# The inner dimension of two FFNs in 45 tiles of 126 instead of 44 tiles of 128

## The chip, the core and the metric

The kernel runs on one core of one Trainium2 chip. The metric is the device time of one execution in microseconds (us). The kernel before the change took 2538.53 us, the median of three runs (2537.65 to 2539.0). In the views of the profile PE is TensorE's matmuls, PEld its weight loads, DVE is VectorE, ACT is ScalarE, POOL is GpSimd and SP the engine that issues most of the DMAs.

## The reference

One layer of a decoder for 320 tokens (256 of a prompt and 8 sequences of 8): a half-step FFN, a mixer of two kinds of heads, cross attention over 256 memory tokens, a second half-step FFN and a last norm. The change touches the two FFNs:

```python
def swiglu_ffn(x, wg, wu, wd):
    return (jax.nn.silu(x @ wg) * (x @ wu)) @ wd

def block(x, mk, mv, s0, buf0, lb, p):
    ...
    x = x + FFN_RES * swiglu_ffn(rmsnorm(x, n_f1), f1_g, f1_u, f1_d)
    m, s_new, buf_new = mixer(rmsnorm(x, n_mix), s0, buf0, lb, w_in, gnorm, conv_w, conv_b, ln_g, ln_b, w_out)
    x = x + m
    x = x + cross_attn(rmsnorm(x, n_xa), mk, mv, xa_q, xa_o)
    x = x + FFN_RES * swiglu_ffn(rmsnorm(x, n_f2), f2_g, f2_u, f2_d)
    return x, s_new, buf_new
```

x has 2048 columns (D_MODEL), the inner dimension of the FFNs (D_FF) is 5632, and everything is float32.

## The kernel before

Activations lie transposed: the 2048 columns of x are 16 blocks (KT) of 128 partitions by 320 tokens (T), the tiles xs. Every large product is made of three matmuls on float32r operands: a number is split into a high part (a cast to float32r) and a low part (the rest), and high x high, high x low and low x high are added up in PSUM. `mm3` issues the three (lines 206 to 208): the stationary operand is a 128 x 128 block of weights, its high part `whi` twice and its low part `wlo` once, and the moving operand is the high or low part of the activations, 128 x 320. Each matmul has its own weight load.

The weights of the whole program lie in one array in DRAM in the order in which they are used, cut into units of 128 x 1024, that is eight blocks. `unit` hands out the next one; `fetch` keeps four in work: a DMA into one of three buffers `raw` (512 KB, issued by SP), a cast to `whi` on ACT (line 136) and a subtraction to `wlo` on DVE (line 137).

`ffn` computes one FFN in parts of the inner dimension, PARTS = [8, 8, 8, 8, 8, 4] tiles of 128, 44 (FT) in all. For each tile, `strip` runs 16 blocks of gate weights (two units, 48 matmuls) against the pairs `xg` into a PSUM tile `acc`, `gate` scales it and applies Silu, a second strip does the same for the up weights, and `up` multiplies both and splits the product into the pair `hh`, `hl`. When the tiles of a part are there, the down projection runs for each of the 16 blocks n of the output over the part's tiles, and a DVE instruction (line 323) adds half of it to xs[n]. In the last part the first two blocks n are begun without the last tile and finished when it is there, which gives the last tile's gate and up time. The first five strips of the first FFN are run together by `first_strips` while x arrives, block by block over all five.

The order on each engine comes from the scheduler of the framework, with priority for the fetches; `first_strips` and PE in the end of the first FFN stand in the order in which they are written. There (`close`) the 16 tiles of the memory tokens are prepared between the tiles of the last part; they take pairs of the same 16 buffers as `hh`.

On the host, `strips` cuts gate and up weights into blocks, `downs` the down weights, and `ffn_groups` puts them in the order of use.

Of the kernel before, what the change touches and what calls it, by code (L numbers as in the profile page):

```python
# [10 lines left out]
F32 = mybir.dt.float32  # L11
# [3 lines left out]
ALU = mybir.AluOpType  # L15
AX = mybir.AxisListType

P = 128
DM = 2048
KT = DM // P  # L20
FF = 5632
FT = FF // P
NP = 256
NS = 64
T = NP + NS
# [10 lines left out]
XCUTS = ((0, 1), (1, 2), (2, 4), (4, 6), (6, 8), (8, 12), (12, 16))  # L36
HEAD = 5
EPS = 1e-6
PARTS = [8, 8, 8, 8, 8, 4]
LEVELS = [(0, T), (1, T), (2, T), (4, T), (8, NP), (16, NP), (32, NP)]  # L40

V_NORM = {"ffn1": 0, "mix": 16, "xattn": 32, "mem": 48, "ffn2": 64, "final": 80}
# [9 lines left out]

CRATE = 1.5
HRATE = 1.15


OUTPARTS = [list(range(7)), list(range(8, 16)) + [7]]
# [22 lines left out]
def hymba(tc, A, O):  # L80
# [3 lines left out]
    def tl(pool, shape, dt, tag, bufs):  # L84
        count[0] += 1
        return pool.tile(shape, dt, tag=tag, name=f"{tag}_{count[0]}", bufs=bufs)
# [9 lines left out]
    with (  # L96
# [8 lines left out]
        def acc():  # L105
            return tl(pp, [P, 512], F32, "acc", 4)
# [93 lines left out]
                mms[0] -= pace[0]  # L200
                pump()

        def mm3(out, w, kk, xh, xl, first, last):
            hi = w[0][:, kk * P : (kk + 1) * P]
            lo = w[1][:, kk * P : (kk + 1) * P]
            nc.tensor.matmul(out, hi, xh, start=first, stop=False)  # L206
            nc.tensor.matmul(out, hi, xl, start=False, stop=False)  # L207
            nc.tensor.matmul(out, lo, xh, start=False, stop=last)  # L208
            tick(1)

        def strip(xg, ps, between=None):
            for half in range(2):
                if half and between is not None:
                    between()
                w = unit()
                for kk in range(8):
                    k = half * 8 + kk
                    mm3(ps, w, kk, *xg[k], k == 0, k == KT - 1)


        def root(r, ps, n):
# [42 lines left out]

        def ffn(pool, xg, root_of, done, setup=None, head=None, close=None):
            def gate(pg, r):
                t = tl(pool, [P, T], F32, "fa", 2)
                nc.vector.tensor_tensor(t, pg[:, :T], r, ALU.mult)  # L268
                nc.scalar.activation(t, t, AF.Silu)  # L269
                nc.vector.tensor_tensor(t, t, r, ALU.mult)  # L270
                return t

            def up(pu, t):
                hp = pair("h")
                h = tl(pool, [P, T], F32, "fb", 2)
                nc.vector.tensor_tensor(h, pu[:, :T], t, ALU.mult)  # L276
                split(*hp, h)
                return hp

            for pi, np_ in enumerate(PARTS):  # L280
                last_part = pi == len(PARTS) - 1
                hs = []
                if pi == 0 and head is not None:
                    r, strips_ = head(xg)
                    for pg, pu in strips_:
                        t = gate(pg, r)
                        if pu is None:
                            pu = acc()
                            strip(xg, pu[:, :T])
                        hs.append(up(pu, t))  # L290
                while len(hs) < np_:
                    if last_part and close is not None:
                        close(len(hs))
                    pg = acc()
                    strip(xg, pg[:, :T])
                    if pi == 0 and not hs:
                        r = root_of()
                    t = gate(pg, r)
                    pu = acc()
                    strip(xg, pu[:, :T])  # L300
                    hs.append(up(pu, t))
                w = None
                if last_part and close is not None:
                    close(np_)
                late = []
                for n in range(KT):
                    if n * np_ % 8 == 0:
                        w = unit()
                    ps = acc()
                    if last_part and n < 2:  # L310
                        late.append(ps)
                        for kk in range(np_ - 1):
                            mm3(ps[:, :T], w, n * np_ + kk, *hs[kk], kk == 0, False)
                        if n == 0:
                            continue
                        for m, ps in enumerate(late):
                            mm3(ps[:, :T], w, m * np_ + np_ - 1, *hs[np_ - 1], False, True)
                            nc.vector.scalar_tensor_tensor(xs[m], ps[:, :T], 0.5, xs[m], ALU.mult, ALU.add)
                            done(m)
                        continue  # L320
                    for kk in range(np_):
                        mm3(ps[:, :T], w, n * np_ % 8 + kk, *hs[kk], kk == 0, kk == np_ - 1)
                    nc.vector.scalar_tensor_tensor(xs[n], ps[:, :T], 0.5, xs[n], ALU.mult, ALU.add)  # L323
                    if last_part:
                        done(n)
                if pi == 0 and setup is not None:
                    setup(pool)

# [2 lines left out]
        def first_strips(xg):  # L331
            with tc.manual_schedule():
# [67 lines left out]
                for i in range(nblocks):  # L400
                    while work and work[0][0] <= i + 8:
                        _, _, f, args = work.pop(0)
                        f(*args)
                    if i % 8 == 0:
                        w = units[upos[0]]
                        units[upos[0]] = None
                        upos[0] += 1
                    k = i // HEAD
                    mm3(ps[i % HEAD][:, :T], w, i % 8, *xg[k], k == 0, k == KT - 1)
                while work:  # L410
                    _, _, f, args = work.pop(0)
                    f(*args)
# [58 lines left out]
        with phase("ffn1") as fp:  # L471
            stat1 = Stat(True)


            mpairs = []

            def mem_tiles(n):
                for k in range(len(mpairs), n):
                    mx = mems[k // 4][:, k % 4, :]
                    nc.vector.scalar_tensor_tensor(mx, mx, norm("mem", k), rmem, ALU.mult, ALU.mult)  # L480
                    mpairs.append(pair("h", MEM))
                    split(*mpairs[k], mx)

            order = contextlib.ExitStack()

            def close(n):
                if n == PARTS[-1]:
                    order.enter_context(tc.manual_schedule(engines={mybir.EngineType.PE}))
                else:
                    mem_tiles(3 * n)  # L490

            ffn(fp, [], None, lambda n: stat1.add(xs[n]), setup, first_strips, close)
            mem_tiles(KT)
            pv = [acc() for _ in range(4)]
            xg = []
            for k in range(KT):
                mh, ml = mpairs[k]
                w = unit()
                for mt in range(2):
                    a = slice(mt * P, (mt + 1) * P)  # L500
                    for i in range(2):
                        b = slice(i * 512, i * 512 + 512)
                        ps = pv[2 * i + mt]
                        nc.tensor.matmul(ps, mh[:, a], w[0][:, b], start=k == 0, stop=False)  # L504
                        nc.tensor.matmul(ps, mh[:, a], w[1][:, b], start=False, stop=False)  # L505
                        nc.tensor.matmul(ps, ml[:, a], w[0][:, b], start=False, stop=k == KT - 1)  # L506
                if k == 2:
                    r = stat1.rstd()
                    for n in range(KT):
                        t = tl(fp, [P, T], F32, "gt", 2)  # L510
                        nc.vector.scalar_tensor_tensor(t, xs[n], norm("mix", n), r, ALU.mult, ALU.mult)
                        hp = pair("xg")
                        split(*hp, t)
                        xg.append(hp)
            for mt in range(2):
                nc.scalar.copy(vM[:, mt, :], pv[mt])
            nc.sync.dma_start(O["mv"], vM)
            kM = tl(fp, [P, 2, 512], F32, "t4k", 2)
            for mt in range(2):
                nc.scalar.copy(kM[:, mt, :], pv[2 + mt])  # L520
            nc.sync.dma_start(O["mk"], kM)
            order.close()
# [559 lines left out]


def downs(w):
    out = []
    f0 = 0
    for np_ in PARTS:
        a = w[f0 * P : (f0 + np_) * P].reshape(np_, P, KT, P).transpose(2, 1, 0, 3)
        g = 16 // np_
        a = a.reshape(KT // g, g, P, np_ * P).transpose(0, 2, 1, 3)  # L1090
        out.append(a.reshape(KT // g, P, 2048))
        f0 += np_
    return out


def ffn_groups(w_gate, w_up, w_down, head=0):
    g, u, d = strips(w_gate), strips(w_up), downs(w_down)
    out = []
    both = [w[j] for j in range(FT) for w in (g, u)]
    if head:  # L1100
# [124 lines left out]
```

## Time and profile before

| | |
|---|---|
| median of three runs | 2538.53 us |
| the profiled execution | 2535.14 us |
| its span | 2533.0 us |
| granted clock of TensorE over the span | 0.997 |
| DMA, mean over the span | 155 GB/s |
| weight units of 512 KB, issue to landing | 3.7 us |

All rows of a profile here are from one execution. The first FFN runs up to about 938 us, the second from about 1595 us; between them lie the keys and values of the memory, the mixer and the cross attention. In a row of a group, the figures after the names are the stationary operand (rows*columns) and the output's or input's shape, the count after x, the busy time in us and the mean of one in ns, and behind the last bar the engine's idle time before such instructions with what ended it. Starts in a timeline are us from the span's start. A row of the busy time by stretches has, after its length, busy us and count (x) of PE, PEld, DVE, ACT and POOL, then the granted clock, the DMA share and GB/s.

### The profile page before, as it was taken

How to read it: one execution, taken by the hardware profiler on the slowest of the kernel's cores; microseconds unless marked ns; L12 is line 12 of the kernel's file. 1: busy time of each engine (PE TensorE's matmuls, PEld its weight loads, DVE VectorE, ACT ScalarE, POOL GpSimd, SP SyncE). 2: the span in 40 equal slices, each digit the busy share in tenths (PEclk: the TensorE clock that was granted, in tenths of full speed). 3: DMA queues.
4: the chain of work that ended last, by engine and by line, in shares of the span. 5: the costliest groups of instructions: out<-in, count | busy, mean ns of one | idle time of the engine just before them, and what ended most of it. 6: DMA issues, size and time to landing. Idle time of an engine off the chain costs nothing.

```text
span 2533.0 us, 41707 instructions
## 1 busy us (share of the span) xinstructions
PE 2511.5 (99%) x17268; PEld 2481.3 (98%) x17268; DVE 1486.1 (59%) x2141; ACT 1050.8 (41%) x1546; POOL 78.3 (3%) x90
## 2 busy tenths in 40 slices
PE   9999999999999999999999999999999999999998
PEld 9999999999999999999999899999999999999998
DVE  7655444444444567999998766644444444444444
ACT  6433333333333355555665555433333333333334
POOL 0100000000000020000000021100000000000002
PEclk9999999999999999999999999999999999999999
DMA  6544444444444446444444454444444444444443
GB/s 222 201 149 149 150 150 150 150 150 150 151 149 150 150 152 224 145 167 148 151 155 135 145 189 165 150 150 150 150 151 150 150 149 151 150 149 150 150 149 112
DMA packets 111356, 393.16 MB, mean 155 GB/s; under 512 B 12608, under 2 KB 16704, under 8 KB 111168
## 3 DMA queue, kind: packets, MB, share of 16 engines
q1 hardware_dynamic: 111024, 390.35, 47.1%
q8 instruction: 135, 2.21, 0.3%
q14 instruction: 53, 0.43, 0.0%
q10 hardware_dynamic: 144, 0.16, 0.0%
HBM read 380.71 MB, written 9.76 MB: 154 GB/s over the span
## 4 chain that ended last, share of the span: by engine, by line
PE 97%; DVE 1%; issue 0%; ACT 0%; DMA 0%; DVEq 0%; SPq 0%; POOLq 0%; ACTq 0%
PE acc L206 31%; PE acc L207 31%; PE acc L208 31%; PE acc L504 1%; PE acc L505 1%; PE acc L506 1%; PE sm L705 0%; DVE wlo L137 0%; PE sm L774 0%; DVE xgl L262 0%; DMA raw<-in_w 0%; PE sm L679 0%; DVE x L1018 0%; PE sm L788 0%; PE sm L813 0%
## 5 line engine op out<-in xcount | busy, mean ns | idle before, releaser
L136 ACT CAST whi<-raw 128x1024 fp32r<-128x1024 f32 (+1 forms) x692 | 722.5, 1045 | 1325.6 <-PE acc L207 947.8
L137 DVE TENSOR_TENSOR wlo<-raw,whi 128x1024 fp32r<-128x1024 f32 (+1 forms) x692 | 847.0, 1224 | 521.1 <-ACT whi L136 519.2
L206 PE MATMUL acc<-xgh,whi 128*128 128x320 f32 x3616 | 1127.4, 312 | 0.7 <-DVE x L1018 0.4
L208 PE MATMUL acc<-xgh,wlo 128*128 128x320 f32 x3616 | 1118.5, 309 | 0.2 <-DVE wlo L137 0.2
L207 PE MATMUL acc<-xgl,whi 128*128 128x320 f32 x3616 | 1117.7, 309 | 0.5 <-DVE xgl L262 0.4
L206 PEld LDWEIGHTS acc<-xgh,whi 128*128 128x128 f32 x3616 | 679.1, 188 | 6.0 <-issue 4.0
L207 PEld LDWEIGHTS acc<-xgl,whi 128*128 128x128 f32 x3616 | 679.1, 188 | 1.4 <-DVE xgl L262 1.0
L208 PEld LDWEIGHTS acc<-xgh,wlo 128*128 128x128 f32 x3616 | 678.7, 188 | 1.6 <-DVE wlo L137 1.3
L206 PE MATMUL acc<-hh,whi 128*128 128x320 f32 x1728 | 537.3, 311 | 0.0
L207 PE MATMUL acc<-hl,whi 128*128 128x320 f32 x1728 | 535.6, 310 | 0.9 <-DVE hl L137 0.9
L208 PE MATMUL acc<-hh,wlo 128*128 128x320 f32 x1728 | 535.1, 310 | 0.0
L207 PEld LDWEIGHTS acc<-hl,whi 128*128 128x128 f32 x1728 | 325.5, 188 | 2.2 <-DVE hl L137 1.5
L206 PEld LDWEIGHTS acc<-hh,whi 128*128 128x128 f32 x1728 | 325.4, 188 | 1.2 <-DVE wlo L137 0.3
L208 PEld LDWEIGHTS acc<-hh,wlo 128*128 128x128 f32 x1728 | 325.5, 188 | 0.2 <-issue 0.2
L323 DVE SCALAR_TENSOR_TENSOR x<-acc,x 128x320 f32<-128x320 f32 x188 | 92.2, 491 | 226.3 <-PE acc L208 226.2
L244 POOL TENSOR_TENSOR ssq<-ssq,sq 128x320 f32<-128x320 f32 x57 | 61.6, 1080 | 1834.5 <-ACT sq L242 932.5
L582 DVE SCALAR_TENSOR_TENSOR hl<-u,vec,hl 128x256 f32<-128x256 f32 x240 | 114.2, 480 | 3.2
L276 DVE TENSOR_TENSOR fb<-acc,fa 128x320 f32<-128x320 f32 x87 | 42.7, 491 | 106.0 <-PE acc L208 106.0
L268 DVE TENSOR_TENSOR fa<-acc,r 128x320 f32<-128x320 f32 x87 | 42.7, 491 | 104.9 <-PE acc L208 104.8
L270 DVE TENSOR_TENSOR fa<-fa,r 128x320 f32<-128x320 f32 x88 | 43.1, 491 | 1.0 <-ACT fa L269 1.0
L137 DVE TENSOR_TENSOR hl<-fb,hh 128x320 fp32r<-128x320 f32 x88 | 42.5, 484 | 0.0
L269 ACT ACTIVATE fa<-fa 128x320 f32<-128x320 f32 x88 | 40.9, 466 | 2.5 <-DVE fa L268 2.5
(257 smaller groups left out, 1071.7 us busy)
## 6 DMA issues: line engine op xcount, KB each, us to landing
raw<-in_w SPq DMA_DIRECT2D x687, 512.0 KB, 3.7
t<-in_s SPq DMA_DIRECT2D x8, 512.0 KB, 4.2
out_ss<-t SPq DMA_DIRECT2D x8, 512.0 KB, 5.1
kv<-in_ck SPq DMA_DIRECT2D x8, 512.0 KB, 5.7
kv<-in_cv SPq DMA_DIRECT2D x8, 512.0 KB, 5.7
mem<-in_mem SPq DMA_DIRECT2D x4, 512.0 KB, 5.8
out_conv<-u SPq DMA_DIRECT2D x8, 167.0 KB, 3.1
x<-in_x SPq DMA_DIRECT2D x2, 640.0 KB, 7.4
```

Source lines behind the costliest of these rows:

```text
L136: nc.scalar.copy(hi, src)
L137: nc.vector.tensor_tensor(lo, src, hi.bitcast(F32), ALU.subtract)
L206: nc.tensor.matmul(out, hi, xh, start=first, stop=False)
L207: nc.tensor.matmul(out, hi, xl, start=False, stop=False)
L208: nc.tensor.matmul(out, lo, xh, start=False, stop=last)
L244: nc.gpsimd.tensor_tensor(self.total, self.total, s, ALU.add)
L268: nc.vector.tensor_tensor(t, pg[:, :T], r, ALU.mult)
L269: nc.scalar.activation(t, t, AF.Silu)
L270: nc.vector.tensor_tensor(t, t, r, ALU.mult)
L276: nc.vector.tensor_tensor(h, pu[:, :T], t, ALU.mult)
L323: nc.vector.scalar_tensor_tensor(xs[n], ps[:, :T], 0.5, xs[n], ALU.mult, ALU.add)
L582: nc.vector.scalar_tensor_tensor(dw[:, :NP], u[:, j : j + NP], cw, dw[:, :NP], ALU.mult, ALU.add)
```

## The change

The inner dimension is cut into 45 tiles of 126 (HT), 5670 in all, of which the last 38 are zeros. The array in DRAM keeps blocks of 128 x 128: on the host each block of gate and up weights gets two columns of zeros, each block of down weights two rows. The gate and up strips load only the first 126 columns of a block (`cols=HT`), so that their outputs have 126 partitions, and so have the operations of `gate` and `up` on DVE and ACT. The down projection loads the first 126 rows and all 128 columns of a block (`rows=HT`). The last part has 5 tiles instead of 4; as 5 does not divide 8, `down_order` writes down the order of the blocks, host and kernel both follow it, and a unit is taken every eight blocks.

```diff
-FT = FF // P
+HT = 126
+FT = -(-FF // HT)
...
-PARTS = [8, 8, 8, 8, 8, 4]
+PARTS = [8, 8, 8, 8, 8, 5]
...
+def down_order(pi):
+    np_ = PARTS[pi]
+    behind = 2 if pi == len(PARTS) - 1 else 0
+    order = [(n, kk) for n in range(behind) for kk in range(np_ - 1)] + [(n, np_ - 1) for n in range(behind)]
+    return order + [(n, kk) for n in range(behind, KT) for kk in range(np_)]
...
-        def mm3(out, w, kk, xh, xl, first, last):
-            hi = w[0][:, kk * P : (kk + 1) * P]
-            lo = w[1][:, kk * P : (kk + 1) * P]
+        def mm3(out, w, kk, xh, xl, first, last, rows=P, cols=P):
+            hi = w[0][:rows, kk * P : kk * P + cols]
+            lo = w[1][:rows, kk * P : kk * P + cols]
...
-        def strip(xg, ps, between=None):
+        def strip(xg, ps, between=None, cols=P):
...
-                    mm3(ps, w, kk, *xg[k], k == 0, k == KT - 1)
+                    mm3(ps[:cols], w, kk, *xg[k], k == 0, k == KT - 1, cols=cols)
...
-                t = tl(pool, [P, T], F32, "fa", 2)
-                nc.vector.tensor_tensor(t, pg[:, :T], r, ALU.mult)
+                t = tl(pool, [HT, T], F32, "fa", 2)
+                nc.vector.tensor_tensor(t, pg[:HT, :T], r[:HT], ALU.mult)
...
-                    strip(xg, pg[:, :T])
+                    strip(xg, pg[:, :T], cols=HT)
...
+                open_ = {}
+                for i, (n, kk) in enumerate(down_order(pi)):
+                    if i % 8 == 0:
+                        w = unit()
+                    if kk == 0:
+                        open_[n] = acc()
+                    mm3(open_[n][:, :T], w, i % 8, *hs[kk], kk == 0, kk == np_ - 1, rows=HT)
+                    if kk == np_ - 1:
+                        nc.vector.scalar_tensor_tensor(xs[n], open_.pop(n)[:, :T], 0.5, xs[n], ALU.mult, ALU.add)
+                        if last_part:
+                            done(n)
...
-                    mm3(ps[i % HEAD][:, :T], w, i % 8, *xg[k], k == 0, k == KT - 1)
+                    mm3(ps[i % HEAD][:HT, :T], w, i % 8, *xg[k], k == 0, k == KT - 1, cols=HT)
...
-                    mem_tiles(3 * n)
+                    mem_tiles(min(3 * n, KT - PARTS[-1]))
...
+def hidden(w):
+    w = np.pad(w, ((0, 0), (0, FT * HT - FF))).reshape(DM, FT, HT)
+    return np.pad(w, ((0, 0), (0, 0), (0, P - HT))).reshape(DM, FT * P)
...
-    g, u, d = strips(w_gate), strips(w_up), downs(w_down)
+    g, u, d = strips(hidden(w_gate)), strips(hidden(w_up)), downs(w_down)
```

On PE the number of matmul rows goes from 16713 to 17001, on SP from 773 rows to 785. Two places on PE show how. The first is the start of the first FFN, two blocks of its first strips (xgh and xgl are the high and low part of block 0 of x, whi and wlo those of the first unit; the last figure is the output's shape). Before:

```order
L206 MATMUL sm_114<-xgh_119,whi_123 128x320
L207 MATMUL sm_114<-xgl_120,whi_123 128x320
L208 MATMUL sm_114<-xgh_119,wlo_124 128x320
L206 MATMUL sm_115<-xgh_119,whi_123 128x320
L207 MATMUL sm_115<-xgl_120,whi_123 128x320
```

and now:

```order
L215 MATMUL sm_114<-xgh_119,whi_123 126x320
L216 MATMUL sm_114<-xgl_120,whi_123 126x320
L217 MATMUL sm_114<-xgh_119,wlo_124 126x320
L215 MATMUL sm_115<-xgh_119,whi_123 126x320
L216 MATMUL sm_115<-xgl_120,whi_123 126x320
```

The order is the same; outputs have 126 partitions because the stationary operands have 126 columns.

The second is the start of the down projection in the last part of the first FFN (acc_8752 before and acc_8897 now are the output's block 1, hh and hl with four numbers the tiles of the part, whi_8635 a unit of weights). Before, from block 1's third tile on:

```order
L206 MATMUL acc_8752<-hh_8581,whi_8635 128x320
L207 MATMUL acc_8752<-hl_8582,whi_8635 128x320
L208 MATMUL acc_8752<-hh_8581,wlo_8636 128x320
L206 MATMUL acc_8742<-hh_8728,whi_8635 128x320
L207 MATMUL acc_8742<-hl_8729,whi_8635 128x320
L208 MATMUL acc_8742<-hh_8728,wlo_8636 128x320
L206 MATMUL acc_8752<-hh_8728,whi_8635 128x320
```

and now, from block 1's third tile on:

```order
L215 MATMUL acc_8897<-hh_8581,whi_8777 128x320
L216 MATMUL acc_8897<-hl_8582,whi_8777 128x320
L217 MATMUL acc_8897<-hh_8581,wlo_8778 128x320
L215 MATMUL acc_8897<-hh_8728,whi_8777 128x320
L216 MATMUL acc_8897<-hl_8729,whi_8777 128x320
L217 MATMUL acc_8897<-hh_8728,wlo_8778 128x320
L215 MATMUL acc_8884<-hh_8870,whi_8812 128x320
L216 MATMUL acc_8884<-hl_8871,whi_8812 128x320
L217 MATMUL acc_8884<-hh_8870,wlo_8813 128x320
```

The tile hh_8728 was the part's last and is now the last but one; the matmuls that need the last tile (hh_8870) begin after 24 of the down projection instead of 18, and with a new unit (whi_8812).

More of the change, by code (lines that the diff above doesn't have):

```diff
@@ L266, in gate @@
             def gate(pg, r):
-                t = tl(pool, [P, T], F32, "fa", 2)
-                nc.vector.tensor_tensor(t, pg[:, :T], r, ALU.mult)
+                t = tl(pool, [HT, T], F32, "fa", 2)
+                nc.vector.tensor_tensor(t, pg[:HT, :T], r[:HT], ALU.mult)
                 nc.scalar.activation(t, t, AF.Silu)
-                nc.vector.tensor_tensor(t, t, r, ALU.mult)
+                nc.vector.tensor_tensor(t, t, r[:HT], ALU.mult)
                 return t
             def up(pu, t):
-                hp = pair("h")
-                h = tl(pool, [P, T], F32, "fb", 2)
-                nc.vector.tensor_tensor(h, pu[:, :T], t, ALU.mult)
+                hp = tuple(z[:HT] for z in pair("h"))
+                h = tl(pool, [HT, T], F32, "fb", 2)
+                nc.vector.tensor_tensor(h, pu[:HT, :T], t, ALU.mult)
                 split(*hp, h)
@@ L288, in ffn @@
                             pu = acc()
-                            strip(xg, pu[:, :T])
+                            strip(xg, pu[:, :T], cols=HT)
                         hs.append(up(pu, t))
@@ L299, in ffn @@
                     pu = acc()
-                    strip(xg, pu[:, :T])
+                    strip(xg, pu[:, :T], cols=HT)
                     hs.append(up(pu, t))
-                w = None
                 if last_part and close is not None:
                     close(np_)
-                late = []
-                for n in range(KT):
-                    if n * np_ % 8 == 0:
+                open_ = {}
+                for i, (n, kk) in enumerate(down_order(pi)):
+                    if i % 8 == 0:
                         w = unit()
[L309 to L325, printed above, removed]
+                    if kk == 0:
[5 more added lines that the diff above has]
+                            done(n)
                 if pi == 0 and setup is not None:
@@ L1084, in downs @@
 def downs(w):
+    w = np.pad(w, ((0, FT * HT - FF), (0, 0))).reshape(FT, HT, KT, P)
+    w = np.pad(w, ((0, 0), (0, P - HT), (0, 0), (0, 0)))
     out = []
     f0 = 0
[L1087 to L1091, printed above, removed]
+    for pi, np_ in enumerate(PARTS):
+        a = np.concatenate([w[f0 + kk, :, n] for n, kk in down_order(pi)], axis=1)
+        out.append(a.reshape(P, -1, 2048).transpose(1, 0, 2))
         f0 += np_
     return out
+def hidden(w):
+    w = np.pad(w, ((0, 0), (0, FT * HT - FF))).reshape(DM, FT, HT)
+    return np.pad(w, ((0, 0), (0, 0), (0, P - HT))).reshape(DM, FT * P)
 def ffn_groups(w_gate, w_up, w_down, head=0):
-    g, u, d = strips(w_gate), strips(w_up), downs(w_down)
+    g, u, d = strips(hidden(w_gate)), strips(hidden(w_up)), downs(w_down)
     out = []
```

## The prediction

> **What bounds the kernel now.** I read the page's busy shares and its chain of work first.
>
> ```profile
> PE 2511.5 (99%) x17268; PEld 2481.3 (98%) x17268; DVE 1486.1 (59%) x2141; ACT 1050.8 (41%) x1546; POOL 78.3 (3%) x90
> PE 97%; DVE 1%; issue 0%; ACT 0%; DMA 0%; DVEq 0%; SPq 0%; POOLq 0%; ACTq 0%
> ```
>
> PE is busy for 99% of the span, and the chain that ended last is PE for 97% of it: what counts is how many matmuls there are and how far apart they start. The groups tell which ones.
>
> ```profile
> L206 PE MATMUL acc<-xgh,whi 128*128 128x320 f32 x3616 | 1127.4, 312 | 0.7 <-DVE x L1018 0.4
> L206 PEld LDWEIGHTS acc<-xgh,whi 128*128 128x128 f32 x3616 | 679.1, 188 | 6.0 <-issue 4.0
> L206 PE MATMUL acc<-hh,whi 128*128 128x320 f32 x1728 | 537.3, 311 | 0.0
> ```
>
> A mean of 312 ns is a matmul from its start to its modelled end, and matmuls overlap. The price of one is the distance between starts, which the busy time by stretches gives where PE does nothing else (one stretch in each FFN):
>
> ```profile
> 100.00:900.00 800.00, 800.00 (x5456) 799.95 (x5455) 395.13 (x483) 272.36 (x316) 0.00 (x0) 1.00 0.46 150
> 1700.00:2500.00 800.00, 800.00 (x5456) 799.83 (x5455) 384.77 (x459) 269.33 (x310) 1.93 (x2) 1.00 0.46 150
> ```
>
> 800/5456 = **146.63 ns** for a load of 128 columns and its matmul of 320, gate, up and down alike, with the granted clock at 1.00. What is it made of? The timeline shows the same float32r pair with 512 moving columns:
>
> ```profile
> 959.54 0.39 PE L506 MATMUL acc<-whi,hl 128*128 128x512 f32 x1
> ...
> 961.58 0.39 PE L506 MATMUL acc<-whi,hl 128*128 128x512 f32 x1
> ```
>
> Nine pairs lie between these starts: 2.04/9 = 226.7 ns. So 192 more columns cost 80.0 ns, 0.417 ns each; 320 columns are 133.4 ns, and **13.3 ns is fixed in every pair**, the worth of 32 columns. Plain f32 matmuls, with the same 128-column loads (each recorded matmul passes its columns at two column-times), do not show it:
>
> ```profile
> 1531.71 0.81 PE L939 MATMUL sm<-pT,vM 128*128 128x256 f32 x3
> 1532.36 1.03 PE L918 MATMUL sm<-kT,q 128*128 128x256 f32 x4
> ...
> 1550.74 0.81 PE L939 MATMUL sm<-pT,vM 128*128 128x256 f32 x3
> 1551.38 1.03 PE L918 MATMUL sm<-kT,q 128*128 128x256 f32 x4
> ```
>
> Three starts apart is 0.65 and 0.64 us, 216.7 and 213.3 ns each, against 2 x 256 x 0.417 = 213.5: a fixed part of 0 to 3.2 ns, about 2. Nor do float32r pairs have it at half the clock:
>
> ```profile
> 1404.00:1407.00 3.00, 3.00 (x12) 2.80 (x12) 0.92 (x2) 0.99 (x3) 0.00 (x0) 0.50 0.04 15
> 1404.51 0.47 PE L207 MATMUL acc<-hl,whi 128*128 128x320 f32 x1
> ...
> 1406.38 0.47 PE L208 MATMUL acc<-hh,wlo 128*128 128x320 f32 x1
> ```
>
> There the granted clock was 0.50, and seven pairs took 1.87 us: 267.1 ns, 320 columns at 0.835 and no fixed part. So the 13.3 ns is no property of the array. It looks like a collision: a float32r stream at full clock takes a column every 0.417 ns, and something in each pair takes 32 of its slots; a stream that leaves every second slot free (f32, or half clock) hides it. The load stands beside each matmul, and 128 columns taken four at a time are 32 slots.
>
> **The change, part by part.** Gate and up: 2 FFNs x 44 tiles x 2 strips x 16 blocks x 3 = 8448 pairs become 8640, with loads of 126 columns. Down: 2 x 44 x 16 x 3 = 4224 pairs become 4320, whose loads keep 128 columns but have 126 rows. If nothing else changes, that is 288 x 146.63 = +42.2 us.
>
> *The price of a pair with 126 columns* decides the sum, and no float32r load in this trace has fewer than 128. Bounds from the rows: 133.4 ns is the stream alone, 136.6 the stream with the largest f32 remainder, 146.63 is today's price. Upwards, the nearest row is the step from a float32r matmul to a load of 32 columns that goes to one quarter of the array (`tile_position` in the code), where nothing overlaps:
>
> ```profile
> 1059.24 0.31 PE L208 MATMUL acc<-xgh,wlo 128*128 128x320 f32 x1
> 1059.48 0.64 PE L759 MATMUL sm<-t,qpad 128*32 128x128 f32 x16
> ```
>
> That is 240 ns. 126 columns still reach into all four quarters, so it is the far end. I take **135.3 ns**, the stream and 2 ns: that the fixed part is worth exactly a quarter of 128 columns, and disappears where the stream has spare slots, fits best with a wide load that a full set of 128 columns gets and a shorter one does not. For it a narrow load must be covered:
>
> ```profile
> L951 PEld LDWEIGHTS sm<-kv,qm 128*32 128x32 f32 x64 | 1.9, 109 | 1.7 <-issue 0.7
> ```
>
> From 32 to 128 columns a load's record grows from 109 to 188 ns, 0.82 ns per column; 126 such columns are 104 ns, under the 133.4 ns of the stream that runs meanwhile. This row also speaks against me: the record of 128 columns is as long as column by column would be, so the wide load is not seen in the load's own record.
>
> The Trainium skill, "TensorE: Matmul & The Clock Gate", section "Weight-path perf modes", has such a mode: fast weight load, on when the number of weights is 128 and the type is not FP32. If float32r counts as another type, its condition falls with 126 columns, as in my forecast. The same page, section "LDWEIGHTS", would then make the load about 105 ns (an estimate, 126 columns at 1.2 per ns), which the trace's 0.82 ns per column agrees with.
>
> So gate and up go from 8448 x 146.63 = 1238.7 to 8640 x 135.3 = 1169.0: **-69.7 us** (-86.1 at 133.4, -58.5 at 136.6).
>
> *Down*: 96 x 146.63 = **+14.1 us**. For 126 rows I take no effect: a load with fewer rows (64, in f32) is recorded about as long as a full one.
>
> ```profile
> L788 PEld LDWEIGHTS sm<-vt,ket 64*128 64x128 f32 x64 | 4.2, 186 | 1.4 <-PE acc L207 0.8 <-issue 0.6
> ```
>
> The end above nothing there is today's 13.3 ns per pair kept, which is what I count; the end below is the fixed part gone here too (a rival).
>
> *The feeding* must stand a faster PE.
>
> ```profile
> L137 DVE TENSOR_TENSOR wlo<-raw,whi 128x1024 fp32r<-128x1024 f32 x686 | 844.0, 1231 | 517.8 <-ACT whi L136 515.8 <-DMA raw<-in_w 1.0
> L136 ACT CAST whi<-raw 128x1024 fp32r<-128x1024 f32 x686 | 719.8, 1050 | 1320.7 <-PE acc L207 947.8 <-issue 343.2 <-PE acc L506 13.2
> L276 DVE TENSOR_TENSOR fb<-acc,fa 128x320 f32<-128x320 f32 x87 | 42.7, 491 | 106.0 <-PE acc L208 106.0
> raw<-in_w SPq DMA_DIRECT2D x687, 512.0 KB, 3.7
> ```
>
> A tile of the inner dimension is 96 pairs, 13.0 us at 135.3. Against it stand four splits of a weight unit and four short operations on DVE, 4 x 1.23 + 4 x 0.49 = 6.9 us, less on ACT, and four units of 512 KB, 161 GB/s. Three raw buffers at 3.7 us from issue to landing plus 2.3 us of splitting supply a unit every 2.0 us, where 3.25 are needed. The 12 added units and the added tile per FFN are hidden behind PE for the same reason; uncovered, the units would be 12 x 2.3 = 28 us of splitting.
>
> ```profile
> 0.00:40.00 40.00, 38.14 (x240) 36.38 (x241) 29.11 (x48) 28.18 (x50) 1.04 (x8) 1.00 0.74 245
> ```
>
> Only at the start, where x arrives beside the weights (245 GB/s, DVE busy for 29 of 40 us), may the first 240 pairs gain nothing: 0 to 240 x 11.3 = 2.7 us lost, I take +1.4.
>
> *The last part of each FFN* (5 tiles, was 4) now runs 24 pairs before the first that needs the last tile, instead of 18. The wait there is small anyway:
>
> ```profile
> L207 PE MATMUL acc<-hl,whi 128*128 128x320 f32 x1728 | 535.6, 310 | 0.9 <-DVE hl L137 0.9
> ```
>
> 0.9 us in the whole span: 0 to -0.9, taken as 0. The y output at the end is untouched.
>
> Sum: -69.7 + 14.1 + 1.4 = **-54.2 us**. The profiled execution took 2535.14 us (span 2533.0), so it becomes 2480.9; the median of the runs, 2538.53, lies 3.4 above it, so I predict **2484.3**. With the ends of these terms the forecast's own range is 2466 to 2497.
>
> **The rivals.**
>
> 1. *The fixed part stays* (slower). The collision may belong to the float32r matmul itself, or to the bytes of the load: 126/128 of 13.3 is 13.1. For it: the load's record, column by column in every row; the f32 pairs, which load the same 128 columns without paying. Against: it does not grow with the 320 or 512 columns streamed, and is worth just 32. Result: +42.2, or +40.5 with 0.2 ns less on 8640: 2579 to 2581. The point from which the change loses is 8640 x price = 1238.7 - 14.1, 141.7 ns: when more than 8.3 of the 13.3 ns remain.
> The Trainium skill's type condition, read with float32r as FP32, gives this one (the loads' records have type f32): no fast mode before, none to lose, and 288 pairs more; it is part of this chance.
>
> 2. *Rows count too*: 126 rows free the down pairs as well: 4320 x 11.3 = -48.8 more, 2435. For it only that the whole array is then not full either; against it the 64-row loads, which look like full ones.
>
> 3. *Part of it goes*, say half (140.0 ns, 8640 x 140.0 = 1209.6, -29.1 + 14.1 + 1.4): 2525. A new wait of the faster stream on a unit of weights would look the same; the margins above speak against it.
>
> 4. *The narrow load is not covered*, 240 ns: 8640 x 240 - 1238.7 + 14.1 = +849, 3387. Against: the place in the array is the same from one pair to the next.
>
> **How the numbers follow.** Forecast 0.54; rival 1 0.36; rival 2 0.05; rival 3 0.04; rival 4 0.01. A measurement of this kernel tells about 0.2%, 5 us, from no change. Faster: 0.54 + 0.05 + 0.03 = 0.62; within 0.2%: 0.01, a part of rival 3; slower 0.37. The cases lie on both sides, so the range must reach from the forecast to rival 1: 2468 to 2583, which leaves out rivals 2 and 4 and the forecast's lowest edge, about 1 in 10. The likeliest case alone is 2466 to 2497.
>
> **What would show it.** In a stretch of gate and up the number of matmuls per us gives the price: 7.39 per us for 135.3 ns, 6.82 for rival 1. Starts in the timeline of a strip should be 0.135 apart, those of down 0.147; down at 0.135 is rival 2. The load's record, now 128*126, should stay near 187 ns if it is read column by column. DMA should rise from 150 to some 160 GB/s in the FFNs, and PE's idle time should stay under some us; if PE waits on DVE wlo or ACT whi, the feeding is the bound (rival 3). The forecast is wrong if the price per pair with 126 columns is 141.7 ns or more.

## The result, and the profile after

| | before | after |
|---|---|---|
| median, same chip | 2538.15 us (4 runs, 2537.65 to 2539.0) | 2570.34 us (4 runs, 2569.75 to 2571.01) |
| profiled execution, its span | 2535.14, 2533.0 us | 2571.01, 2569.2 us |
| granted clock over the span | 0.997 | 0.997 |

The change makes the kernel slower by 32.2 us: a ratio of 1.0129, with a 95% interval of 1.0114 to 1.0144. The prediction forecast 2484.3 us; the time lies inside its range (2468 to 2583), on the side of its first rival. The page of the kernel after, its counts, busy times and the chain that ended last:

```profile
span 2569.2 us, 42366 instructions
PE 2545.9 (99%) x17556; PEld 2517.3 (98%) x17556; DVE 1505.1 (59%) x2161; ACT 1065.9 (41%) x1562; POOL 78.9 (3%) x90
PE 96%; DVE 2%; DMA 1%; issue 1%; ACT 0%; DVEq 0%; SPq 0%; ACTq 0%
```

PE has the 288 matmuls more that were counted (17556 against 17268) and is still what the time is made of. Outside its busy time it has 23.3 us (2569.2 - 2545.9), before 21.5. So nothing new is waited for, and the price of a pair must have stayed. The busy time by stretches shows it (us, then busy us and count of PE, PEld, DVE, ACT, POOL, the granted clock, DMA share, GB/s). First the long stretches of the two FFNs, then part 2 of the first FFN and part 2 of the second, each gate and up alone:

```profile
100.00:900.00 800.00, 800.00 (x5508) 799.94 (x5507) 399.25 (x488) 274.65 (x318) 0.00 (x0) 1.00 0.47 151
1720.00:2520.00 800.00, 800.00 (x5456) 800.00 (x5455) 383.37 (x454) 266.01 (x302) 0.00 (x0) 1.00 0.47 150
181.00:288.00 107.00, 107.00 (x743) 107.00 (x743) 59.26 (x80) 41.00 (x51) 0.00 (x0) 1.00 0.47 150
1780.00:1888.00 108.00, 108.00 (x738) 108.00 (x737) 52.10 (x63) 38.14 (x47) 0.00 (x0) 1.00 0.46 150
```

A stretch also counts matmuls that are in flight at its edges, about two, which matters in a short one: with two taken off, part 2 of the second FFN has 108/736 = **146.7 ns** a pair with 126 columns, as before the change; part 2 of the first has 107/741 = **144.4 ns**. The long stretch of the second FFN holds 5456 matmuls, exactly as many as before. DMA stays at 150 GB/s instead of rising to 160, because PE is not faster.

So there are two rhythms. The timelines of a strip in each (starts in us, duration, line, names and shapes) show them; in the first FFN:

```profile
230.79 0.31 PE L215 MATMUL acc<-xgh,whi 128*126 128x320 f32 x1
...
232.24 0.31 PE L216 MATMUL acc<-xgl,whi 128*126 128x320 f32 x1
```

Ten pairs in 1.45 us: 145 ns, within the 10 ns of a start's last digit the 144.4 of the stretch. And in the second, eight pairs in 1.17 us, 146 ns:

```profile
1829.80 0.31 PE L215 MATMUL acc<-xgh,whi 128*126 128x320 f32 x1
...
1830.97 0.31 PE L217 MATMUL acc<-xgh,wlo 128*126 128x320 f32 x1
```

Down, with 126 rows and 128 columns, has 21 pairs in 3.08 us: 146.7 ns, the price of before, as the prediction's step had it (lines 215 to 217 are the former 206 to 208).

```profile
129.78 0.31 PE L217 MATMUL acc<-hh,wlo 126*128 126x320 f32 x1
...
132.86 0.31 PE L217 MATMUL acc<-hh,wlo 126*128 126x320 f32 x1
```

The groups of operations give the loads' records (count, busy us and mean ns before the last bar), and the wait of the last part:

```profile
L216 PEld LDWEIGHTS acc<-xgl,whi 128*126 128x126 f32 x2848 | 530.2, 186 | 1.2 <-DVE xgl L271 1.0
L217 PEld LDWEIGHTS acc<-hh,wlo 126*128 126x128 f32 x1440 | 270.3, 188 | 0.0
L216 PE MATMUL acc<-hl,whi 126*128 126x320 f32 (+1 forms) x1760 | 545.4, 310 | 0.9 <-DVE hl L146 0.9
```

A load of 126 columns is recorded at 186 ns against 188 for 128: two columns fewer shorten the record by about two columns' worth (0.82 ns each in the prediction), and nothing jumps, as it would if a wide load had been lost. The sum is then: 288 x 146.67 = +42.2 us; in the first FFN's parts 2 to 6, 37 tiles x 2 strips x 48 = 3552 pairs cost about 2.2 ns less, -7.8; PE's time without work +1.8. That makes +36.2, and the two spans differ by 36.2 (the two profiled executions by 35.9, the medians by 32.2).

### The profile page after: what moved, and what is told of

Same layout as the page of the kernel before. It is cut to its first block, busy times and chain, and to the rows that moved or that the text cites. A ratio compares the mean times of both kernels' runs of the same rounds, so it can differ in the third digit from the quotient of the medians.

```text
span 2569.2 us, 42366 instructions
## 1 busy us (share of the span) xinstructions
PE 2545.9 (99%) x17556; PEld 2517.3 (98%) x17556; DVE 1505.1 (59%) x2161; ACT 1065.9 (41%) x1562; POOL 78.9 (3%) x90
## 4 chain that ended last, share of the span: by engine, by line
PE 96%; DVE 2%; DMA 1%; issue 1%; ACT 0%; DVEq 0%; SPq 0%; ACTq 0%
PE acc L215 30%; PE acc L216 30%; PE acc L217 30%; DVE wlo L146 1%; PE acc L504 1%; PE acc L503 1%; PE acc L502 1%; DMA t4k<-in_msk 0%; PE sm L703 0%; PE sm L772 0%; DVE xgl L271 0%; PE sm L677 0%; DMA mem<-in_mem 0%; DVE x L1016 0%; ACT whi L145 0%
## 5 line engine op out<-in xcount | busy, mean ns | idle before, releaser
L215 PE MATMUL acc<-xgh,whi 128*126 128x320 f32 (+1 forms) x3680 | 1145.2, 311 | 0.4 <-DVE x L1016 0.4
L216 PE MATMUL acc<-xgl,whi 128*126 128x320 f32 (+1 forms) x3680 | 1135.8, 309 | 0.5 <-DVE xgl L271 0.4
L217 PE MATMUL acc<-xgh,wlo 128*126 128x320 f32 (+1 forms) x3680 | 1132.5, 308 | 1.9 <-DVE wlo L146 1.9
L215 PEld LDWEIGHTS acc<-xgh,whi 128*126 128x126 f32 (+1 forms) x3680 | 686.7, 187 | 5.3 <-issue 4.0
L216 PEld LDWEIGHTS acc<-xgl,whi 128*126 128x126 f32 (+1 forms) x3680 | 686.8, 187 | 1.4 <-DVE xgl L271 1.0
L217 PEld LDWEIGHTS acc<-xgh,wlo 128*126 128x126 f32 (+1 forms) x3680 | 685.1, 186 | 2.6 <-DVE wlo L146 2.4
L215 PE MATMUL acc<-hh,whi 126*128 126x320 f32 (+1 forms) x1760 | 547.1, 311 | 0.0
L216 PE MATMUL acc<-hl,whi 126*128 126x320 f32 (+1 forms) x1760 | 545.4, 310 | 0.9 <-DVE hl L146 0.9
L217 PE MATMUL acc<-hh,wlo 126*128 126x320 f32 (+1 forms) x1760 | 545.2, 310 | 0.0
L216 PEld LDWEIGHTS acc<-hl,whi 126*128 126x128 f32 (+1 forms) x1760 | 331.7, 188 | 1.7 <-DVE hl L146 1.1
```

## The experiments

Three readings of the 13.3 ns stood against each other: a wide load that only a full 128 columns get ("wide load", the prediction's), a part that goes with the number of columns loaded ("share"), and a part that belongs to the float32r matmul whatever is loaded ("matmul"). The time of the kernel before is given from the same chip each time: 2537.72 us (13 runs) beside the first four kernels, 2536.80 (7 runs) beside the other four.

**A sweep of columns.** The kernel before, its six parts of each FFN with different numbers of columns in gate and up (and as many rows in down). The rest of each tile is left out, so the loops and counts are those of before (the output is then another; this kernel only prices the pairs).

```diff
+COLS = [126, 127, 124, 120, 112, 96]
...
+                ht = COLS[pi]
...
-                    strip(xg, pg[:, :T])
+                    strip(xg, pg[:, :T], cols=ht)
...
```

> The kernel before (44 tiles) with loads of 126, 127, 124, 120, 112 and 96 columns in the gate and up strips of the six parts of each FFN; the rest of each tile of 128 is left out of the FFN. The number of pairs is that of before. Three theories of the 13.3 ns that every float32r pair costs over its stream. Share: the load takes slots of the stream in proportion to its columns; a pair then costs 146.5 at 126 and 127, 146.3 at 124, 145.8 at 120, 145.0 at 112 and 143.4 at 96, alike in both FFNs. Matmul: it belongs to the matmul; 146.67 in all twelve parts. Rhythm: load and stream fall into one of a few repeating patterns; the prices are a few steps (146.67, 144.5, perhaps lower ones with fewer columns), and the same count can cost differently in the two FFNs.

2534.52 us. The stretches inside strips, in order of time the fifth part of the first FFN (112 columns), its last (96), and the first part of the second FFN (126):

```profile
690.00:795.00 105.00, 105.00 (x718) 105.00 (x717) 49.57 (x60) 36.91 (x45) 0.00 (x0) 1.00 0.46 149
856.00:906.00 50.00, 50.00 (x343) 50.00 (x342) 26.45 (x38) 20.01 (x30) 0.00 (x0) 1.00 0.46 148
1600.00:1696.00 96.00, 96.00 (x667) 96.00 (x666) 49.41 (x61) 36.68 (x45) 0.00 (x0) 1.00 0.47 153
```

With two taken off: 105/716 = 146.6 ns at 112 columns, 50/341 = 146.6 at 96, and 96/665 = 144.4 at 126. The other parts, 127, 124 and 120 columns, stand at 146.67 too, down at 146.7 with 96 to 127 rows. The first part of the first FFN, with 126 columns too, has both prices in turn, 31/211 = 146.9 and 39/270 = 144.4 ns:

```profile
43.00:74.00 31.00, 31.00 (x213) 31.00 (x213) 22.11 (x37) 23.68 (x31) 5.09 (x3) 1.00 0.71 238
81.00:120.00 39.00, 39.00 (x272) 39.00 (x271) 21.69 (x27) 15.28 (x19) 0.00 (x0) 1.00 0.58 188
```

The price does not know the columns, but for 126 alone; while the loads do:

```profile
L208 PEld LDWEIGHTS acc<-xgl,whi 128*127 128x127 f32 x512 | 96.0, 187 | 0.0
L208 PEld LDWEIGHTS acc<-xgl,whi 128*112 128x112 f32 x512 | 88.8, 174 | 0.0
L208 PEld LDWEIGHTS acc<-xgl,whi 128*96 128x96 f32 x256 | 41.2, 161 | 0.0
```

A load of 96 columns is 27 ns shorter than one of 128 and its pair is no cheaper. "Wide load" and "share" fall.

**The count alone.** The kernel after, but its strips load all 128 columns (the last two are zeros); the outputs of `gate` and `up` keep 126 partitions.

```diff
...
-                    strip(xg, pg[:, :T], cols=HT)
+                    strip(xg, pg[:, :T])
...
```

> The changed kernel with loads of all 128 columns (two of them zeros) in the gate and up strips, everything else as changed. If only the count of pairs and the columns matter, all 12960 pairs of the FFNs cost 146.65 and the time is 2538.2 + 42.2 = 2580.4, 10 above the changed kernel. If the 126 columns gave nothing and something else made up the difference, it is the changed kernel's 2570.3.

2578.85 us (4 runs, 2578.19 to 2580.78): a ratio of 1.0167 (1.0152 to 1.0183), +41.1 us. The same stretch of the first FFN as above:

```profile
181.00:288.00 107.00, 107.00 (x732) 107.00 (x731) 59.06 (x79) 40.87 (x51) 0.00 (x0) 1.00 0.46 150
```

732 matmuls instead of 743: 107/730 = 146.6 ns. The 42.2 us of 288 pairs at the old price lie inside the interval of this ratio; nothing else is needed. The 126 columns themselves give back 8.5 us (2578.85 - 2570.34), where the forecast wanted 96 (42.2 + 54.2).

**Does something set the faster rhythm?** In the kernel after, the first FFN changes to 144.4 ns behind its first part and the second FFN does not. There a plain f32 matmul for the memory stands between part 1 and part 2, so one such matmul was added behind part 1 of the second FFN.

```diff
+                if pi == 0 and setup is None:
+                    ps = sm()
+                    nc.tensor.matmul(ps[:, :MEM], ones, at[0][:, :MEM], start=True, stop=True)
```

> The changed kernel with one plain f32 matmul of 256 columns more, after the first part of the second FFN (the first FFN has such a one at that place, and its strips cost 144.5 from there on). Rhythm: the strips of parts 2 to 6 of the second FFN go from 146.67 to 144.5, 74 strips x 48 x 2.17 = 7.7 us less, and the time is about 2563. Share and matmul: no change, 2570 to 2571.

Four runs: 2577.16, 2570.65, 2579.71 and 2572.21 us, a ratio of 1.0148 (1.0127 to 1.0168); the lowest lies almost 8 us above the 2563 expected. In the profiled one (2577.16) the same two stretches of parts 2 as above are both slow:

```profile
181.00:288.00 107.00, 107.00 (x732) 107.00 (x731) 58.66 (x80) 39.58 (x50) 0.00 (x0) 1.00 0.46 148
1780.00:1888.00 108.00, 108.00 (x738) 108.00 (x737) 50.98 (x61) 37.01 (x45) 0.00 (x0) 1.00 0.46 148
```

The added matmul does not bring the rhythm to the second FFN, and the first FFN does not have it in part 2, without any change of its own. It had it earlier: the end of part 1, here and then in the kernel after:

```profile
82.00:121.00 39.00, 39.00 (x272) 39.00 (x271) 21.67 (x27) 15.60 (x19) 0.00 (x0) 1.00 0.58 189
82.00:121.00 39.00, 39.00 (x268) 39.00 (x268) 21.12 (x27) 15.43 (x19) 0.00 (x0) 1.00 0.58 185
```

That is 39/270 = 144.4 ns here and 39/266 = 146.6 in the kernel after. Between these stretches and part 2 lie the down projection of part 1 and the same plain f32 matmul; one execution came out of them slower, the other faster. My theory, that such a matmul starts the faster rhythm, fell.

**The address.** In the kernel before two tiles of 1 column share one, which is meant to put every tile behind them 32 bytes lower (no view shows the addresses).

```diff
+        table = cp.tile([P, 1], F32, name="table")
...
-                table = cp.tile([P, 1], F32, name="table")
...
-                    warm = cp.tile([P, 1], F32, name="warm")
-                    nc.scalar.activation(warm, stat1.total[:, :1], AF.Sqrt)
+                    nc.scalar.activation(table, stat1.total[:, :1], AF.Sqrt)
```

> The kernel before with all tiles of weights and activations 32 bytes lower in each partition, so that every operand of the float32r matmuls starts at a multiple of 64 bytes instead of 32 above one. If the fixed part comes of operands that straddle 64 bytes, one step of 6.7 ns less per pair, 16000 pairs, about 2432. If the place does not matter, 2538.

2537.67 us (10 runs), a ratio of 1.0001 (0.9991 to 1.001). A stretch of the first FFN:

```profile
100.00:900.00 800.00, 800.00 (x5455) 799.95 (x5454) 394.54 (x482) 271.64 (x315) 0.00 (x0) 1.00 0.46 150
```

146.7 ns a pair, as before: if the tiles moved as meant, 32 bytes in the place of the operands make no difference.

**Another type.** The sweep again with bfloat16 in place of float32r in every split (the subtractions then read the high part without a bitcast). The memory's keys and values, which have no columns left out, then stand 4.5e-6 (relative) off the reference instead of 4.5e-7: it is another precision.

```diff
-F32R = mybir.dt.float32r
+F32R = mybir.dt.bfloat16
...
+COLS = [128, 126, 127, 124, 112, 96]
...
```

> The kernel before with all high and low parts in bf16 instead of float32r (so the products keep fewer digits), and loads of 128, 126, 127, 124, 112 and 96 columns in the gate and up strips of the six parts of each FFN; the rest of each tile of 128 is left out. The mechanism of my forecast, a wide load for a full set of 128 columns, is asked for in a type in which such a load may exist: if it takes slots of the stream, the strips with 128 columns and all down pairs cost 146.7 and the strips with fewer columns 135 to 136. Reading theory (a matmul's operand is read in 0.417 ns per float32r column plus 13.3 ns, beside an array that takes a column in 0.417 ns; the longer of the two is the price): with half the bytes to read the array is the longer one, and all pairs cost 133.4 plus 2 to 3 ns whatever the columns. If the 13.3 ns belongs to every load and matmul at full clock, all stay at 146.7.

2374.66 us. Stretches of part 2 (126 columns) and of the last part (96) of the first FFN, and of part 3 of the second (127):

```profile
175.00:270.00 95.00, 95.00 (x702) 95.00 (x700) 55.34 (x77) 37.28 (x45) 0.00 (x0) 1.00 0.50 161
797.00:845.00 48.00, 48.00 (x356) 43.47 (x354) 26.82 (x38) 20.86 (x31) 0.00 (x0) 1.00 0.50 160
1810.00:1910.00 100.00, 100.00 (x738) 100.00 (x737) 51.38 (x61) 36.84 (x45) 0.00 (x0) 1.00 0.50 161
```

95/700, 48/354 and 100/736: 135.7, 135.6 and 135.9 ns. That is the price that the forecast took for 126 columns (135.3), but at 96 columns as at 127, and at 128 below. The loads' records differ:

```profile
L208 PEld LDWEIGHTS <-whi 128*128 128x128 bf16 x1920 | 188.6, 98 | 73.4 <-issue 3.9
L208 PEld LDWEIGHTS <-whi 128*127 128x127 bf16 x512 | 70.5, 138 | 0.0
```

Here is the wide load: 98 ns for a full 128 columns, 138 for 127. In bf16 it exists, and it changes nothing between the starts of two matmuls. The Trainium skill, "TensorE: Matmul & The Clock Gate", section "Weight-path perf modes", has fast weight load when the number of weights is 128 and the type is not FP32: the records agree, if float32r counts as FP32 (187 and 188 ns).

**bfloat16 with nothing left out.** The kernel before with the type alone changed.

> The same with all 128 columns everywhere, nothing left out; high and low parts have 8 bits each. Reading theory: 16128 pairs of 320 columns and 192 of 512 cost 11 ns less, about 178 us less: 2360. If the type does not matter: 2538.

2373.52 us (4 runs, 2372.68 to 2374.71): a ratio of 0.9357 (0.9343 to 0.9371), 163 us faster than before and 197 faster than after. A stretch of the first FFN with 128 columns, and the page:

```profile
100.00:800.00 700.00, 700.00 (x5154) 504.26 (x5153) 370.50 (x448) 253.05 (x287) 0.00 (x0) 1.00 0.50 162
span 2370.7 us, 41549 instructions
PE 2336.2 (99%) x17268; PEld 1671.7 (71%) x17268; DVE 1478.5 (62%) x2141; ACT 1047.7 (44%) x1546; POOL 76.8 (3%) x90
PE 85%; DVE 10%; ACT 2%; issue 1%; DMA 1%; SPq 0%; DVEq 0%; POOLq 0%; ACTq 0%
```

700/5152 = 135.9 ns: 10.8 ns of the 13.3 are gone in every pair. With 16128 such pairs (3 x 5376) and 192 of 512 columns, some 11 ns each, 177 us were to be had. Most of the missing 14 is new idle time: PE lacks work for 34.5 us instead of 21.5, and the chain that ended last runs over DVE for 10% of the span instead of 1%.

**Other counts, float32r again.** The first sweep with 125, 126, 122, 118, 104 and 80 columns.

> As the first run with columns 125, 126, 122, 118, 104 and 80 in the six parts (float32r, the rest of each tile left out). Rhythm of 126 alone: 144.4 may show in the second part of either FFN, all other counts 146.67. If other counts near a multiple of 8 less 2 have it as well, 122, 118 show 144 to 145 in some strips.

2538.16 us. Part 2 of the first FFN (126 columns) and its last part (80):

```profile
181.00:288.00 107.00, 107.00 (x732) 107.00 (x731) 58.66 (x79) 39.47 (x49) 0.00 (x0) 1.00 0.46 148
856.00:906.00 50.00, 50.00 (x343) 50.00 (x342) 26.65 (x37) 20.04 (x30) 0.00 (x0) 1.00 0.46 151
```

146.6 ns each, and at all counts, this time at 126 as well. So down to 80 columns nothing is gained, and 126 may run at either price.

**The kernel after once more.**

> The changed kernel again, unchanged. If the step of 144.4 is entered by chance in each execution, the times spread from 2563 (all strips in it after the first) to 2580 (none), and the profile shows other strips in it than the first one did; if the program sets it, times stay within 2 us of 2570.

Four runs: 2570.38, 2572.9, 2570.74 and 2580.49 us, a ratio of 1.0149 (1.0131 to 1.0168). The profiled one (2570.38) has both rhythms where the first execution had them, part 2 of the first FFN and part 2 of the second:

```profile
181.00:288.00 107.00, 107.00 (x743) 107.00 (x742) 59.00 (x80) 40.99 (x51) 0.00 (x0) 1.00 0.47 151
1780.00:1888.00 108.00, 108.00 (x738) 108.00 (x738) 51.33 (x63) 37.87 (x46) 0.00 (x0) 1.00 0.46 149
```

The run of 2580.49, which was not profiled, lies where the kernel with 128 columns loaded lies (2578.19 to 2580.78): it would be an execution without the faster rhythm. So each half of the expectation came out in part: the times spread as they would by chance, and the profiled execution has the rhythm just where the first one had it. What is shown is that the time of the same program varies by 10 us; that the rhythm makes this difference is an inference from the times.

## Why the prediction was wrong

*What bounds the kernel* was right: PE is 99% busy before and after, and the time is the number of pairs times their price.

*The price of a pair* was right as a reading of before (133.4 ns of stream and 13.3 fixed), and wrong in the one step that decided the sum: "I take 135.3 ns", because the fixed part "fits best with a wide load that a full set of 128 columns gets". Measured: 146.7 or 144.4 ns. At the first the change costs 42.2 us, at the second 8640 pairs would still lie 2.7 ns above the break-even of 141.7 that rival 1 named. The sweeps show that the fixed part depends neither on the columns (80 to 128, but for the 2.2 ns at 126) nor on the rows (80 to 128), and the bfloat16 kernel shows that it depends on the type of the operands. The fit had rested on one equality, 13.3 ns = 32 columns = 128/4; as the part is the same with 80 columns, it is no quarter of what is loaded. The row that the prediction quoted against itself, the load's record growing by 0.82 ns per column up to 188 ns at 128, was the direct evidence and said that no wide load took place. I gave the coincidence 0.54 and the row 0.36. The cover of a narrow load was mis-sized too: "104 ns" counts the columns alone and leaves out the part of a record that does not grow with them. The load of 126 is recorded at 186 ns, longer than the 133.4 of the stream, and still does not set the price.

That the time lies inside the range owes nothing to the forecast. The range was drawn from the forecast to rival 1, and 2570 lies 73 us above the upper end of the one (2497) and 9 below the lower end of the other (2579).

*Rival 1* was right in what matters, 288 pairs at the old price. Its reason "belongs to the float32r matmul itself" agrees with all runs but was not separated from the load that each matmul brings; its other reason, that the part goes by the bytes of the load, falls with the sweep. Its time, 2579 to 2581 us, is what the kernel with 128 columns loaded takes; the kernel after is 8.5 us below it for the rhythm that neither case foresaw.

*Rows* (rival 2) and *half* (rival 3) fall with down's 146.7 ns and with the sweeps; the *uncovered load* (rival 4) did not show.

*Down* (+14.1), *the feeding* (DVE 59%, the units hidden, DMA 150 GB/s) and *the last part* (0.9 us before and after) went as worked out. The feeding was not tried hard here, since PE did not get faster; the bfloat16 kernel tried it at 135.9 ns and 162 GB/s, and the FFN's stretch has PE busy throughout, as the prediction worked out for 161. At *the start* there was no gain to lose.

What the 13.3 ns is made of is only bounded. It is there with 320 and 512 columns, absent at half the clock and in plain f32 (rows in the prediction), and 2.5 ns in bfloat16, where the output in PSUM is the same f32 tile as before. One explanation agrees with these rows and forecast the price of the bfloat16 sweep: reading a float32r operand takes some 13 ns per matmul beside the time of its columns, while the array, which works at the same time, needs the columns' time alone, and the longer of the two is the price. At half the clock or with two column-times for a column the array is the longer one, and so it is with half the bytes to read. This is argued, not shown: whether it is the bytes, or something else in which float32r differs, was not tried, nor whether the load beside the matmul takes part. The second rhythm, which shows only with 126 columns loaded, is not explained by it and speaks for some part of the load.

## What to carry to other kernels

Before a kernel is made to pay more instructions for a cheaper one, put the sizes into one sweep: one run with six column counts decided between the readings that go by the columns, where the change would have needed 5 ns a pair to break even. A constant that equals a neat share of a size (here 128/4) is weak evidence; where a record of the thing itself (here the load's) speaks against it, the record counts for more. Where a fixed part per matmul vanishes at half the clock, as here, try the operands' type as well as their shape: with bfloat16 pairs this kernel takes 0.9357 of its time, at fewer digits.

## What the runs showed of the hardware that was not expected

A float32r pair with exactly 126 columns has a second rhythm, 144.4 ns instead of 146.7. It showed in parts of four of the five profiled executions that had such pairs (after twice, the first sweep, the kernel with the added matmul), not in the second sweep, and at none of the eleven other counts tried from 80 to 128. Once entered behind the first part it lasted to the end of the first FFN, and a second execution of the same program had it in the same place. Changes that can be placed lie near a break in the row of pairs (the plain f32 matmul between parts 1 and 2; in the first sweep a wait of PE behind which 144.4 ns begins), but the same break left one execution faster and another slower. What decides it, and why at 126 alone, stays open. The wait in the first sweep, its length and what ended it in brackets:

```profile
79.68 0.41 PE L209 MATMUL acc<-xgh,wlo 128*126 128x320 f32 x1 [1.04 <-DVE wlo L138]
```

In bfloat16 a full set of 128 columns is loaded in 98 ns and one of 127 in 138, and both pairs take 135.8 ns: the load's length, up to 188 ns, was in no sweep here what set the distance between matmuls.
